# First phase of a two-layer encoder kernel: products from a host-transposed x, with the norm's row factor applied on the way out

## The chip, the cores and the metric

The kernel runs as one program on one core of a Trainium2 chip. The metric is the device time of one execution in microseconds (us). The engines named here are PE (TensorE, matrix products), ACT (ScalarE), DVE (VectorE), POOL (GpSimd) and SP (SyncE, which issues DMA transfers). A number such as L89 is a line of the kernel file.

## The reference, cut to what matters

Two layers over x of 256 rows and 1024 columns, float32. What the first phase computes is the RMSNorm ahead of the mixer and the first columns of the combined projection, q and k of the first head slot (three attention groups of one head each, 128 wide):

```python
for l in range(DEPTH):
    u = rms_norm(x, norm_mix_pre[l])          # x * rsqrt(mean(x*x) + eps) * gain
    m = hybrid_mixer(u, pos, w_in[l], ...)    # proj = u @ w_in; attention, Hyena branch, gates
    x = x + rms_norm(m, norm_mix_post[l])
    u = rms_norm(x, norm_ffn_pre[l])
    x = x + rms_norm(swiglu(u, w_gate_up[l], w_down[l]), norm_ffn_post[l])
```

The factor `rsqrt(mean(x*x) + eps)` is one number per row of x, so it is also one number per row of `u @ w`. The Hyena branch needs filters made by a small network with two sines, which don't depend on x: `h = sin(fr1*(z@w1+b1)); h = sin(fr2*(h@w2+b2)); h @ w3`.

## The kernel before, in words

Every product of the projections is made of three: weights and activations are split into a high part (ACT copies into a narrower format, `hi_of`, L86) and a low part (a subtraction, `lo_of`, L89, on DVE or POOL), and `mm3` (L80) multiplies high by high, high by low, low by high into one PSUM bank. Weights come in pieces of 128x768 or 128x1024 (`raw`, L140), one DMA each on SP's queue. `split_hi` makes `whi` of a piece on ACT, `split_lo` makes `wlo` of it on DVE (every fifth on POOL). Four buffers hold the newest `whi` and `wlo`; a further piece can be split only when PE has finished with an older one.

x sits in two tiles of 128 rows, X0 and X1. In the first phase x_rstd takes the sums of squares of a tile on ACT (L352) and the row factor on POOL (L359, L360); `pre_b` makes u = x * factor * gain on DVE (L385), with the gain row spread over the partitions by two PE products with ones (L813); `to_cols` transposes u on PE (L397) and splits the result into UH and UL, the activations with the model dimension on the partitions. Then `start` (L506) runs eight weight pieces of 128x768: q and k columns of head slot 0. It takes all eight for the rows of X0, makes u of X1 meanwhile, transposes it, and takes the eight pieces again for the rows of X1. Each piece and row tile is six products of 128x384.

After that `mixer` runs `slot(0)`: four more pieces for v of slot 0, each used for both row tiles (twelve products), then `slot(1)` with twelve pieces, and so on. After each piece `tick()` lets one or two background jobs issue their next step. The first two jobs are `filter_mlp` of the two layers. Their steps on PE are fixed by the order of the program: the first products (`fc`, L247) come after the first piece of slot 0, the second ones (`h`, L255) five ticks later, after the first piece of slot 1. Between them lies `sine` (L230): seven instructions on DVE (L233 to L242: `arg` and `kk`) and one on ACT (L243). Both layers' second products stand next to each other on PE.

PE runs in the order in which the program is written. In the block `ordered()` ACT, DVE and POOL do too; elsewhere a list scheduler sets the order of ACT, DVE, POOL and SP once, before the run, and each engine then works through its list in order.

## Time and profile before

| | |
|---|---|
| median of 3 runs | 1116.72 us (1114.47 to 1117.01) |
| the profiled execution | 1115.59 us |
| its span in the trace | 1113.8 us |
| PE busy | 1086.5 us (98%) |
| DVE, ACT, POOL busy | 702.8, 557.3, 411.5 us |
| mean DMA rate | 168 GB/s; 298 GB/s in the first 35 us |

The span runs from the first to the last instruction that the profile holds; the execution is 1.8 us longer. Times in rows are counted from the span's start. A row of the timeline has start, duration, engine, line, operation, output and inputs with shapes; in brackets stands how long the engine was idle before it, and what ended that. Products overlap, so that a row of 0.33 us stands 0.17 us behind the row before it; what a product costs is read from the distance of the starts.

### The profile page before, as it was taken

The numbers are of one execution on the slowest core, as the hardware profiler recorded it, in microseconds if no ns is written. First come the engines' busy times: TensorE is split into PE (matmuls) and PEld (weight loads), VectorE is DVE, ScalarE is ACT, GpSimd is POOL, SyncE is SP. The second block draws the span as 40 slices with busy tenths as digits, with TensorE's granted clock in tenths as the row PEclk, the third lists the DMA queues.
The fourth block names the chain that finished last, engine by engine and source line by source line (L and its number), as shares of the span: only waits on it lengthen the run. The fifth ranks groups of instructions, "written<-read, shape, count | busy, mean of one in ns | idle before, by whom it ended". The sixth has DMA issues, their size and how long they took to land.

```text
span 1113.8 us, 19545 instructions
## 1 busy us (share of the span) xinstructions
PE 1086.5 (98%) x7624; PEld 1039.8 (93%) x7624; DVE 702.8 (63%) x1128; ACT 557.3 (50%) x852; POOL 411.5 (37%) x499
## 2 busy tenths in 40 slices
PE   8999999999999999999989999999999999999997
PEld 7989999999898899998879999999999978999986
DVE  5789975555557756755574777865445676554554
ACT  6655554444545644544455464444355455544442
POOL 3665134478414224201126614455645321111110
PEclk9999999999999999999999999999999999999999
DMA  8575534344446555556654454444455556455662
GB/s 305 163 237 189 174 116 150 112 127 128 147 152 195 184 183 194 178 179 188 189 195 156 148 156 138 137 144 137 119 166 185 155 205 208 145 179 186 196 201 78
DMA packets 59878, 187.21 MB, mean 168 GB/s; under 512 B 6919, under 2 KB 9353, under 8 KB 59786
## 3 DMA queue, kind: packets, MB, share of 16 engines
q1 hardware_dynamic: 59786, 185.96, 52.8%
q8 instruction: 60, 0.98, 0.4%
q14 instruction: 32, 0.26, 0.1%
HBM read 184.89 MB, written 1.05 MB: 167 GB/s over the span
## 4 chain that ended last, share of the span: by engine, by line
PE 82%; POOL 5%; DVE 4%; DMA 3%; issue 3%; ACT 2%; SPq 0%; POOLq 0%; DVEq 0%; ACTq 0%
PE acc L78 79%; DMA gain<-in_gains_dram 2%; DVE wlo L89 1%; ACT whi L86 1%; DMA raw<-in_wa_dram 1%; PE acc L617 1%; POOL wlo L89 1%; ACT jk L352 1%; DVE X L373 1%; PE acc L397 1%; POOL GT L767 1%; PE acc L548 1%; PE acc L647 1%; POOL nr L360 0%; POOL sl L89 0%
## 5 line engine op out<-in xcount | busy, mean ns | idle before, releaser
L86 ACT ACTIVATE whi<-raw 128x1024 fp32r<-128x1024 f32 (+1 forms) x352 | 345.2, 989 | 380.2 <-PE acc L78 292.1
L89 DVE TENSOR_TENSOR wlo<-raw,whi 128x1024 fp32r<-128x1024 f32 (+1 forms) x291 | 346.3, 1195 | 233.4 <-ACT whi L86 232.5
L78 PE MATMUL acc<-UH,whi 128*128 128x256 f32 x1248 | 356.0, 285 | 0.0
L78 PE MATMUL acc<-UH,wlo 128*128 128x256 f32 x1248 | 353.1, 283 | 0.0
L78 PE MATMUL acc<-UL,whi 128*128 128x256 f32 x1248 | 353.0, 283 | 0.0
L89 POOL TENSOR_TENSOR wlo<-raw,whi 128x1024 fp32r<-128x1024 f32 (+1 forms) x61 | 138.4, 2269 | 401.0 <-ACT whi L86 401.0
L78 PEld LDWEIGHTS acc<-UL,whi 128*128 128x128 f32 x1248 | 239.3, 192 | 0.4
L78 PEld LDWEIGHTS acc<-UH,whi 128*128 128x128 f32 x1248 | 239.2, 192 | 0.4
L78 PEld LDWEIGHTS acc<-UH,wlo 128*128 128x128 f32 x1248 | 239.2, 192 | 0.0
L78 PE MATMUL acc<-wlo,UH 128*128 128x384 f32 x448 | 153.7, 343 | 5.4 <-DVE wlo L89 3.5
L78 PE MATMUL acc<-whi,UH 128*128 128x384 f32 x448 | 154.8, 346 | 0.0
L78 PE MATMUL acc<-whi,UL 128*128 128x384 f32 x448 | 152.3, 340 | 0.0
L78 PE MATMUL acc<-whi,hs 128*128 128x512 f32 x352 | 109.0, 389 | 0.0
L78 PEld LDWEIGHTS acc<-wlo,UH 128*128 128x128 f32 x448 | 85.8, 192 | 9.7 <-DVE wlo L89 6.0
L78 PEld LDWEIGHTS acc<-whi,UH 128*128 128x128 f32 x448 | 86.1, 192 | 1.3 <-ACT qk L668 0.4
L78 PEld LDWEIGHTS acc<-whi,UL 128*128 128x128 f32 x448 | 85.9, 192 | 0.2 <-DVE UL L89 0.2
L78 PEld LDWEIGHTS acc<-whi,hs 128*128 128x128 f32 x352 | 66.1, 188 | 13.6
L78 PE MATMUL acc<-wlo,hs 128*128 128x512 f32 x176 | 68.6, 390 | 0.5 <-DVE wlo L89 0.5
L799 DVE TENSOR_TENSOR HF<-acc,silu 128x256 f32<-128x256 f32 x38 | 16.1, 424 | 49.7 <-PE acc L78 49.7
L359 POOL TENSOR_SCALAR nv<-ss 128x1 f32<-128x1 f32 x16 | 4.8, 302 | 108.9 <-ACT jk L352 108.9
L78 PEld LDWEIGHTS acc<-wlo,hs 128*128 128x128 f32 x176 | 33.1, 188 | 7.7 <-DVE wlo L89 0.9
L565 POOL TENSOR_TENSOR t<-t 128x256 f32<-128x256 f32 x32 | 23.6, 741 | 38.8 <-DVE t L562 37.9
(164 smaller groups left out, 1688.3 us busy)
## 6 DMA issues: line engine op xcount, KB each, us to landing
raw<-in_wa_dram SPq DMA_DIRECT2D x240, 512.0 KB, 3.6
raw<-in_wq_dram SPq DMA_DIRECT2D x96, 384.0 KB, 3.2
raw<-in_wg_dram SPq DMA_DIRECT2D x16, 384.0 KB, 3.9
w<-in_w_dram SPq DMA_DIRECT2D x16, 256.0 KB, 4.6
gain<-in_gains_dram SPq DMA_DIRECT2D x7, 512.0 KB, 7.6
dec<-in_dec_dram SPq DMA_DIRECT2D x8, 256.0 KB, 4.2
bb<-in_hyb_dram SPq DMA_DIRECT2D x16, 128.0 KB, 3.7
dftraw<-in_dft_dram SPq DMA_DIRECT2D x3, 256.0 KB, 5.1
```

The lines of the kernel that those rows point to most:

```text
L78: nc.tensor.matmul(o, lT, r, start=start, stop=stop)
L86: return nc.scalar.activation(o, i, AF.Copy)
L89: (eng or nc.vector).tensor_tensor(o, i, h, op=OP.subtract)
L352: nc.scalar.activation(jk, half, AF.Square, scale=D ** -0.5, accum_out=ss[:, h:h + 1])
L373: stt(X[i][:, HALF[h]], t[h], r, X[i][:, HALF[h]], op0=OP.mult, op1=OP.add)
L397: nc.tensor.transpose(t[:, q * P:(q + 1) * P], u[:, h * 512 + q * P: h * 512 + (q + 1) * P], ident)
L548: nc.tensor.transpose(t[:, q * P:(q + 1) * P], eo[:, q // 2, q % 2, :], ident)
L565: ptt(t1[:, 0:256], t1[:, 0:256], t1[:, 256:512], op=OP.subtract)
L617: nc.tensor.transpose(t[:, q * P:(q + 1) * P], qk[i][:, j * 384 + g * P: j * 384 + (g + 1) * P], ident)
L647: nc.tensor.transpose(t[:, q * P:(q + 1) * P], S[:, i * 512 + q * P:i * 512 + (q + 1) * P], ident)
L767: ptt(g0, g0, ct(GT, 8 + c), op=OP.add)
L799: vtt(ct(HF, f), ob, sl, op=OP.mult)
```

## The change

x comes to the chip in two layouts. `xT`, transposed by the host (model dimension on the partitions, 1 MB), and `gT`, the gain as a column, are loaded on ACT's DMA queue at the very start. The first phase forms G = gain * xT, without the row factor, in two splits per 128 rows of the model dimension (ACT L525 for the high part with the gain as a scale operand, DVE L526 for the low part), and runs the eight pieces with G for both row tiles at once. The rows of the results of slot 0 (q, k, and v as well, which also uses G) get the row factor when ACT copies them out of PSUM. X0 and X1 themselves are loaded later, between the weight pieces, and their row factors are taken after pieces 5 and 6.

The normed U, which everything from slot 1 on needs, is built after the eight pieces: two DVE instructions put the row factors on a diagonal (`dg`), one PE product with a 128x128 of ones spreads them (`rb`), eight DVE instructions multiply xT, gain and factor (`ut`, L549), and four pairs of ACT and DVE instructions split them into UH and UL. The 16 transposes of u, the products that spread the gain row, and pre_b of the first phase go away.

```diff
-        grow = bigt(name="grow")[0:1]
-        nc.sync.dma_start(grow, a["gains"][0, 0:1])
-        for s in (slice(0, 512), slice(512, 1024)):
-            nc.sync.dma_start(X[0][:, s], a["x"][0:P, s])
-        ones = cst.tile([1, P], F32, name="ones")
+        gT = cst.tile([P, KT], F32, name="gT")
+        nc.scalar.dma_start(gT, a["gT"])
+        xT = [bigt(name="xT") for h in range(2)]
+        for q in range(4):
+            s = slice((q % 2) * 512, (q % 2) * 512 + 512)
+            nc.scalar.dma_start(xT[q // 2][:, s], a["xT"][:, q * 512:(q + 1) * 512])
+        ones = cst.tile([P, P], F32, name="ones")
...
+        def first_start():
+            G = new_U()
+            o = [[acc() for i in range(2)] for j in range(2)]
+            rs = []
...
+            with ordered():
+                for n in range(START):
+                    for k in (2 * n, 2 * n + 1) if n < 4 else ():
+                        gh = cols(G, k, 0)
+                        nc.scalar.activation(gh, xT_cols(k), AF.Copy, scale=gT[:, k:k + 1])
+                        stt(cols(G, k, 1), xT_cols(k), gT[:, k:k + 1], gh, op0=OP.mult, op1=OP.subtract)
+                    prefetch()
+                    if n == 3:
+                        prefetch()
+                    pc = piece(False)
+                    for i in range(2):
+                        rows_of(G, o[n // 4][i], i, pc, n % 4, 384)
+                    done(pc)
+                    if n in (5, 6):
+                        rs.append(x_rstd(n - 5))
+            dg = f256("dg")
+            for i in range(2):
+                nc.vector.tensor_scalar(dg[:, i * P:(i + 1) * P], ident, rs[i], None, op0=OP.mult)
+            t = acc()
+            mm(t[:, :L], ones, dg, True, True)
+            rb = f256("rb")
+            nc.scalar.activation(rb, t[:, :L], AF.Copy)
+            rb = rb[:, :].rearrange("p (i n) -> p i n", i=2)
+            U = new_U()
+            for k in range(0, KT, 2):
+                ut = t512("ut")
+                v = ut[:, :].rearrange("p (i k n) -> p i k n", i=2, k=2)
+                for q in range(2):
+                    stt(v[:, :, q, :], xT_cols(k + q), gT[:, k + q:k + q + 1], rb, op0=OP.mult, op1=OP.mult)
...
+                hi_of(uh, v)
+                lo_of(ul, v, uh)
+            return U, o, (G, rs)
...
-        def qkv_out(j, i, o, qk, vt):
+        def qkv_out(j, i, o, qk, vt, r=1.0):
             if j < 2:
                 w = slice(j * 384, (j + 1) * 384)
-                nc.scalar.activation(qk[i][:, w], o[:, :384], AF.Copy)
+                nc.scalar.activation(qk[i][:, w], o[:, :384], AF.Copy, scale=r)
...
-                            rows_of(U, o[i], i, pc, kk, 384)
+                            rows_of(G if G and not s else U, o[i], i, pc, kk, 384)
...
         for n in range(START):
             load(n >= RAW)
-            if n == 3:
-                nc.sync.dma_start(X[1], a["x"][P:2 * P, :])
+            if n in (5, 6):
+                nc.sync.dma_start(X[n - 5], a["x"][(n - 5) * P:(n - 4) * P, :])
         load_filter_consts()
         shared[0] = False
-        with ordered():
-            u0 = pre_b(0, x_rstd(0), g)
-            prefetch()
-            U = new_U()
-            to_cols(0, u0, U)
-            prefetch()
-            S = start(U, lambda: pre_b(1, x_rstd(1), g), 3)
+        U, S, first = first_start()
```

What stands in the engines' lists at the two places that the prediction speaks of follows. First DVE in the kernel before, from the last pieces split ahead of the filter networks on; `arg` and `kk` are the sine's tiles, and the number behind a name tells the buffers apart (arg_398 is layer 0's first sine, arg_411 layer 1's):

```order
L89 TENSOR_TENSOR wlo_424<-raw_421,whi_423 128x768
L89 TENSOR_TENSOR wlo_442<-raw_439,whi_441 128x768
L233 TENSOR_SCALAR arg_398<-acc_395,fpar_91 64x256
L235 TENSOR_SCALAR kk_400<-arg_398 64x256
L236 TENSOR_SCALAR kk_400<-kk_400 64x256
L241 SCALAR_TENSOR_TENSOR arg_398<-kk_400,arg_398 64x256 x3
L242 TENSOR_SCALAR arg_398<-arg_398 64x256
L233 TENSOR_SCALAR arg_411<-acc_408,fpar_91 64x256
L89 TENSOR_TENSOR wlo_460<-raw_457,whi_459 128x768
L235 TENSOR_SCALAR kk_413<-arg_411 64x256
L236 TENSOR_SCALAR kk_413<-kk_413 64x256
```

And the same engine in the changed kernel, from the first instruction of layer 0's sine to that of layer 1's second; the eight `ut` instructions of L549 stand directly ahead of these rows:

```order
L235 TENSOR_SCALAR arg_412<-acc_409,fpar_95 64x256
L89 TENSOR_TENSOR wlo_456<-raw_453,whi_455 128x768
L89 TENSOR_TENSOR UL_312<-ut_315,UH_311 128x2x256
L89 TENSOR_TENSOR dft_l_98<-dftraw_338,dft_h_97 128x512
L89 TENSOR_TENSOR UL_312<-ut_320,UH_311 128x2x256
L89 TENSOR_TENSOR UL_314<-ut_325,UH_313 128x2x256
L237 TENSOR_SCALAR kk_414<-arg_412 64x256
L89 TENSOR_TENSOR UL_314<-ut_330,UH_313 128x2x256
L89 TENSOR_TENSOR wlo_474<-raw_471,whi_473 128x768
L238 TENSOR_SCALAR kk_414<-kk_414 64x256
L243 SCALAR_TENSOR_TENSOR arg_412<-kk_414,arg_412 64x256 x3
L89 TENSOR_TENSOR wlo_551<-raw_548,whi_550 128x768
```

Behind these rows come the last step of arg_412, one more wlo, and the seven steps of arg_425, the sine of layer 1. The low parts of U and of the transform tables, which stood ahead of the first sine before, now stand inside it.

The other place is PE's list in the changed kernel at the second products of the filter networks, which stands as before between the first and the second piece of slot 1; h_411 and h_424 are the sines of layer 0 and layer 1:

```order
L78 MATMUL acc<-whi,UL 128x384
L78 MATMUL acc<-h_411,fc 128x256
L78 MATMUL acc<-h_424,fc 128x256
L78 MATMUL acc<-whi,UH 128x384
L78 MATMUL acc<-wlo,UH 128x384
```

Between the first products of these networks and these rows PE has the same four pieces as before. From about the hundredth instruction of each engine on, the lists of ACT, DVE, POOL, SP and PE hold the same operations in the same order as before.

## Rows read from the trace of the kernel before

**Rows 1.** The page's first part, the busy time of PE, and the waits of PE in the first 60 us (who waited for what, us in total, times, longest).

```profile
PE 1086.5 (98%) x7624; PEld 1039.8 (93%) x7624; DVE 702.8 (63%) x1128; ACT 557.3 (50%) x852; POOL 411.5 (37%) x499
...
PE acc L78 <- POOL sl L89: 2.2, 2, 1.7
PE acc L78 <- POOL wlo L89: 0.9, 1, 0.9
```

**Rows 2.** Busy time of the engines in three stretches: the eight pieces of the first phase; slot 0 and the first piece of slot 1 up to the end of the second filter products; the pieces after that. Columns: stretch, length, PE, PEld, DVE, ACT, POOL busy (and instructions), granted clock, DMA share, GB/s.

```profile
9.16:29.33 20.17, 19.30 (x105) 18.33 (x105) 14.44 (x17) 13.03 (x22) 8.33 (x12) 1.00 0.97 334
29.33:42.14 12.81, 12.81 (x70) 11.27 (x69) 9.84 (x18) 8.22 (x12) 9.90 (x21) 1.00 0.46 155
42.14:52.65 10.51, 10.51 (x61) 10.51 (x61) 8.90 (x20) 6.57 (x14) 4.38 (x11) 1.00 0.60 179
```

**Rows 3.** The timeline of the beginning, ACT, DVE and PE.

```profile
4.77 0.61 ACT L352 ACTIVATE jk<-X 128x512 bf16<-128x512 f32 x1
...
6.24 0.84 ACT L86 ACTIVATE whi<-raw 128x768 fp32r<-128x768 f32 x1 [0.77 <-DMA raw<-in_wq_dram]
...
7.88 0.95 DVE L89 TENSOR_TENSOR wlo<-raw,whi 128x768 fp32r<-128x768 f32 x1
...
9.16 0.69 PE L78 MATMUL acc<-whi,UH 128*128 128x384 f32 x1
...
12.03 0.34 PE L78 MATMUL acc<-whi,UL 128*128 128x384 f32 x1
```

**Rows 4.** SP's queue in the same time, one row of issues, and the DMA rate in one window (same columns as rows 2).

```profile
1.14 0.82 SPq L188 DMA_DIRECT2D X<-in_x_dram  x2
...
10.00:12.00 2.00, 2.00 (x7) 1.61 (x7) 1.96 (x3) 2.00 (x3) 0.00 (x0) 1.00 1.03 414
```

**Rows 5.** The timeline of PE and ACT from the first product of slot 0 to the first product after the second filter products, and one wait of PE's weight load between 30 and 45 us (the last row, columns as in rows 1).

```profile
29.33 0.33 PE L78 MATMUL acc<-whi,UH 128*128 128x384 f32 x1
31.24 0.34 PE L78 MATMUL acc<-whi,UL 128*128 128x384 f32 x1
31.51 1.07 PE L78 MATMUL acc<-fc 33*64 33x256 f32 x4
41.04 0.42 ACT L243 ACTIVATE h<-arg 64x256 f32<-64x256 f32 x1 [0.74 <-DVE arg L242]
41.05 1.16 PE L78 MATMUL acc<-h,fc 64*128 64x256 f32 x4
42.14 0.45 PE L78 MATMUL acc<-whi,UH 128*128 128x384 f32 x1
...
PEld acc L78 <- ACT h L243: 0.2, 1, 0.2
```

**Rows 6.** The timeline of DVE over the two first sines, and POOL's one low part in that time.

```profile
31.92 1.10 DVE L89 TENSOR_TENSOR wlo<-raw,whi 128x768 fp32r<-128x768 f32 x1 [3.87 <-ACT whi L86]
32.94 0.53 DVE L233 TENSOR_SCALAR arg<-acc,fpar 64x256 f32<-64x256 f32 x1
33.50 0.30 DVE L235 TENSOR_SCALAR kk<-arg 64x256 f32<-64x256 f32 x1
34.15 1.32 DVE L241 SCALAR_TENSOR_TENSOR arg<-kk,arg 64x256 f32<-64x256 f32 x3
35.51 0.29 DVE L242 TENSOR_SCALAR arg<-arg 64x256 f32<-64x256 f32 x1
37.77 2.86 DVE L241 SCALAR_TENSOR_TENSOR arg<-kk,arg 64x256 f32<-64x256 f32 x3
38.31 2.04 POOL L89 TENSOR_TENSOR wlo<-raw,whi 128x768 fp32r<-128x768 f32 x1 [1.04 <-ACT whi L86]
```

**Rows 7.** Groups of instructions by line and form (count, busy time, mean ns of one, then idle time before them).

```profile
L89 DVE TENSOR_TENSOR UL<-acc,UH 128x512 fp32r<-128x512 f32 x16 | 10.6, 687 | 1.0 <-ACT UH L86 0.6
L315 DVE TENSOR_TENSOR dd<-acc,dec 128x256 f32<-128x256 f32 x64 | 23.0, 411 | 1.0 <-PE acc L78 1.0
L385 DVE SCALAR_TENSOR_TENSOR u<-X,nr,acc 128x512 f32<-128x512 f32 x4 | 2.8, 744 | 6.5 <-POOL nr L360 6.5
L589 ACT ACTIVATE X<-acc,cw 128x256 f32<-128x256 f32 x32 | 17.6, 549 | 0.0
```

**Rows 8.** A place of layer 1 where PE waited: the timeline of PE, and the windows around it (same columns as rows 2).

```profile
576.64 0.34 PE L78 MATMUL acc<-whi,UH 128*128 128x384 f32 x1
578.23 0.57 PE L78 MATMUL acc<-wlo,UH 128*128 128x384 f32 x1 [1.25 <-DVE wlo L89]
578.60 0.52 PE L78 MATMUL acc<-whi,UL 128*128 128x384 f32 x1
581.48 0.49 PE L78 MATMUL acc<-whi,UL 128*128 128x384 f32 x1
...
576.00:578.00 2.00, 0.98 (x6) 0.66 (x4) 2.00 (x3) 1.32 (x4) 0.77 (x1) 1.00 0.60 169
578.00:580.00 2.00, 1.77 (x6) 1.76 (x7) 1.29 (x3) 2.00 (x5) 0.86 (x2) 0.60 0.44 112
580.00:582.00 2.00, 2.00 (x9) 1.91 (x8) 2.00 (x4) 0.32 (x1) 0.00 (x0) 0.55 0.72 206
```

More of the change, by code (lines that the diff above doesn't have):

```diff
@@ L504, in row_proj, with cols, xT_cols, start @@
                 return U, S
-        def start(U, second, at=0):
+        def first_start():
+            G = new_U()
+            o = [[acc() for i in range(2)] for j in range(2)]
+            rs = []
+            def cols(T, k, part):
+                return T[k // 4][part][:, :].rearrange("p (i k n) -> p i k n", i=2, k=4)[:, :, k % 4, :]
+            def xT_cols(k):
+                return xT[k // 4][:, (k % 4) * L:(k % 4 + 1) * L].rearrange("p (i n) -> p i n", i=2)
+            with ordered():
[27 more added lines that the diff above has]
+                    stt(v[:, :, q, :], xT_cols(k + q), gT[:, k + q:k + q + 1], rb, op0=OP.mult, op1=OP.mult)
+                uh, ul = (U[k // 4][part][:, :].rearrange("p (i k n) -> p i k n", i=2, k=4)[:, :, k % 4:k % 4 + 2, :]
+                          for part in range(2))
+                hi_of(uh, v)
+                lo_of(ul, v, uh)
+            return U, o, (G, rs)
+        def start(U, second):
             o = [[acc() for i in range(2)] for j in range(2)]
@@ L513, in start @@
                 rows_of(U, o[n // 4][0], 0, pcs[n], n % 4, 384)
-                if n == at:
+                if n == 0:
                     u1 = second()
@@ L663, in attend, with mixer @@
             yield
-        def qkv_out(j, i, o, qk, vt):
+        def qkv_out(j, i, o, qk, vt, r=1.0):
             if j < 2:
                 w = slice(j * 384, (j + 1) * 384)
-                nc.scalar.activation(qk[i][:, w], o[:, :384], AF.Copy)
+                nc.scalar.activation(qk[i][:, w], o[:, :384], AF.Copy, scale=r)
                 rotary(qk[i][:, w], i)
             else:
-                nc.scalar.activation(vt[:, i * 384:(i + 1) * 384], o[:, :384], AF.Copy)
-        def mixer(l, U, o, K):
+                nc.scalar.activation(vt[:, i * 384:(i + 1) * 384], o[:, :384], AF.Copy, scale=r)
+        def mixer(l, U, o, K, G=None, rs=(1.0, 1.0)):
             qk = [bigt(name="qk") for i in range(2)]
@@ L676, in mixer @@
                 for i in range(2):
-                    qkv_out(j, i, o[j][i], qk, None)
+                    qkv_out(j, i, o[j][i], qk, None, rs[i])
             OT = bigt(F32R, name="OTH"), bigt(F32R, name="OTL")
@@ L695, in slot @@
                     for i in range(2):
-                        qkv_out(j, i, o[i], qk, vt)
+                        qkv_out(j, i, o[i], qk, vt, 1.0 if s else rs[i])
                     tick()
@@ L808, in ffn @@
             return row_proj(l, NF, left, 3, (l + 1, 0) if l + 1 < DEPTH else None)
-        g = [acc() for h in range(2)]
-        for h in range(2):
-            mm(g[h], ones, grow[:, HALF[h]], True, True)
         for n in range(START):
             load(n >= RAW)
-            if n == 3:
-                nc.sync.dma_start(X[1], a["x"][P:2 * P, :])
+            if n in (5, 6):
+                nc.sync.dma_start(X[n - 5], a["x"][(n - 5) * P:(n - 4) * P, :])
         load_filter_consts()
         shared[0] = False
-        with ordered():
-            u0 = pre_b(0, x_rstd(0), g)
-            prefetch()
-            U = new_U()
-            to_cols(0, u0, U)
-            prefetch()
-            S = start(U, lambda: pre_b(1, x_rstd(1), g), 3)
+        U, S, first = first_start()
         shared[0] = True
@@ L832, in trunk @@
         for l in range(DEPTH):
-            U, S = mixer(l, U, S, K)
+            U, S = mixer(l, U, S, K, *(() if l else first))
             if l + 1 < DEPTH:
@@ L899, in _pack @@
     d["x"] = np.ascontiguousarray(i["x"][0][PERM])
+    d["xT"] = np.ascontiguousarray(d["x"].reshape(L, KT, P).transpose(2, 1, 0).reshape(P, KT * L))
+    d["gT"] = np.ascontiguousarray(i["norm_mix_pre"][0].reshape(KT, P).T)
     d["gains"] = np.stack([i["norm_mix_pre"], i["norm_mix_post"], i["norm_ffn_pre"], i["norm_ffn_post"]], 1)
```

## The prediction, on record before the result

> **What bounds the kernel now.** I read the page's first part first: PE is busy 98% of the span [rows 1], so time is won or lost only where PE's stream of products starts earlier, stands still or runs at a lower rate. Then the timeline of the beginning, because the change begins there: PE's first product of the projection starts at 9.16 us, after x, its row sums, u, the transposes and the first split [rows 3]. Then the windows by stage: the eight pieces of the first phase last from 9.16 to 29.33 us, slot 0 with the first piece of slot 1 and the second filter products until 42.14 [rows 2]. In that last stretch the waits matter most. PE's second filter products start at 41.05, and the sine that they read starts at 41.04; the weight load stood only 0.2 us for it [rows 5]. So the sine of the filter networks arrives just in time before: it has no slack. It is made on DVE, which ran through both sines from 31.92 us on, after standing idle for 3.87 us [rows 6].
>
> The question is thus two-sided: how much earlier does PE reach slot 0, and does DVE, which gets the building of U between slot 0's begin and the sines, still deliver the second sine in time?
>
> **Term 1, the first phase.** The first product now needs the first quarter of xT (128x512, 262 KB) and raw piece 0 (128x768, 393 KB), issued at the same time on two queues. Before, the two halves of X0 (524 KB) were there by 4.77 us and those with piece 0 (917 KB) at 6.24 [rows 3]; between these, 655 KB land at 4.77 + 131/393 x 1.47 = 5.3 us. The first issue of X stood at 1.14 us [rows 4], about where ACT's first of xT will stand, behind gT. Two scaled copies on ACT follow: a 128x256 instruction with operands for scale and bias takes 0.55 [rows 7], and the second starts before the first ends, so I take 0.9; then whi 0.84 and wlo 0.95 [rows 3]. The stream of products starts at 5.3 + 0.9 + 0.84 + 0.95 = 8.0 us. It has the same 96 products of 128x384. At full rate they stand (31.24 - 29.33)/11 = 0.174 us apart [rows 5]: 16.7 us. At its beginning PE ran slower before: eight products from 9.16 to 12.03 [rows 3], 2.87 instead of 1.39 us, and nothing has kept PE busy beforehand now, so I add 1.5. The end is 8.0 + 16.7 + 1.5 = 26.2; I use 26.1, as the first of the 96 runs ahead while wlo is made. Gone with the old order are eight transposes between the pieces and the wait of 0.9 for a low part on POOL [rows 1]. Each piece now serves twelve products (2.09 us) at once, so from the second on, a split (0.84 and 0.95) is ready in time even when a quarter of xT and a piece arrive together (655 KB at 414 GB/s [rows 4] is 1.6 us). Against 29.33 this is 3.2 us won. The product that spreads the factors costs about half of the 1.07 for the two first filter products [rows 5], 0.55. Won at the start of slot 0: 2.7 us.
>
> For the low end of this term, the first pair lands with X's second half at 4.77 and the copies take 0.6: 25.2. For the high end, the extra 1 MB of xT is paid in full ahead of the pieces, 1.05 MB at 414 GB/s, 2.5 us: 28.6. I stay near the low end because the later pieces are needed at only 393 KB in 2.09 us, half of what the window shows.
>
> The trace has all transfers on one queue, so it doesn't show how two share. The Trainium skill, DMA: Bandwidth & Descriptors, section "Issuing engines are not separate DMA queues", says that transfers issued by several engines run on the same 16 DMA engines and interleave, and that a second issuer saves only issue time. No run here shows it yet. By that rule the pair lands together, as I reckon; were ACT's queue an addition, the pair could land some 0.5 us earlier.
>
> **Term 2, from slot 0 to the second filter products.** Count from the end of the first phase, T = 26.1. PE itself reaches the second filter products at T + 0.55 + 5 x 2.09 + 1.1 = T + 12.1, or 38.2: five pieces and the first filter products. DVE's list decides whether it may go on. Piece 11's whi can only be made when the last piece of the first phase is finished, for it takes its buffer: whi 0.84, wlo 0.95, T + 1.8. Then, in order: eight `ut` of 128x256 at 0.37 (128x512 takes 0.74 for one [rows 7], so half; 0.41 for another 128x256 instruction is the upper bound), 3.0; first step of the sine 0.53, wlo 0.95; low parts of U and of the tables, five at 0.69 [rows 7], 3.45; one kk 0.30, wlo 0.95, kk 0.30, three steps 1.32, wlo 0.95, 0.29, wlo 0.95 [rows 6]. With 13.0 that is T + 14.8. The second sine adds 0.53 + 0.30 + 0.30 + 1.32 + 0.29 = 2.7: T + 17.5. During such a stretch POOL makes a low part, and beside it the same three steps of a sine took 2.86 instead of 1.32 [rows 6]; the list has one such low part and the rotary steps there again, so I add 1.5: T + 19.0. ACT's sine 0.42, then the second layer's product 0.55 [rows 5]: T + 20.0 = 46.1. Before, the next piece began at 42.14 [rows 5]. So PE is 4.0 us later than before, though it came to slot 0 2.7 us earlier: the wait for the sine eats 6.7 us.
>
> The bounds of this term: no collision with POOL, 0 instead of 1.5; two of them, 3.0; `ut` 0.41 each, 0.3 more. The removed transposes and u give DVE and ACT nothing back here, since both stood ahead of slot 0. The row factor as a scale in the six copies of q, k and v costs less than the 0.55 that an ACT instruction with such operands takes in all [rows 7], and PE's wait covers it. On ACT whi of piece 15 stands behind the two copies of v, which end T + 11.8, so its wlo starts by T + 12.7: within the list's own pace. Rows from PSUM, `dg` and the issue of gT hide under the first phase.
>
> **Term 3, PE's rate after the wait.** Where PE had been busy only 0.98 of 2 us (576 to 578), the granted clock of the next two windows was 0.60 and 0.55, and products stood 0.32 us apart instead of 0.174 until 581.48 [rows 8]: the lower of the two levels, 1.2 GHz. Eleven products cost 11 x 0.146 = 1.6 us. In the wait of term 2 PE does one small product in some 7 us, a longer rest than that. I take 1.6; bounds 0 and 2.2.
>
> The Trainium skill, TensorE: Matmul & The Clock Gate, section "Part 1: The HAM clock gate", says that 1.2 GHz is the default and that only sustained activity releases 2.4. Rows 8 agree (0.55 after a stretch half idle). The rule speaks against this change twice: at the start, where there are no products with ones and no transposes ahead of the stream, and here; by it the sum below holds, without it the sum would be 4.0.
>
> **The sum.** Later: 4.0 + 1.6 = 5.6 us. From there on the lists are the same as before, PE is the bound, and I find nothing that gives time back, except the 2.2 us that PE waits for low parts on POOL between 50 and 60 us [rows 1]: this work hangs on q and k of slot 1, which ACT copies out after the second sines, so I let the wait stand. The profiled execution took 1115.59 us (span 1113.8): 1115.6 + 5.6 = 1121.2. The median of the runs shown is 1.1 above that execution, so I forecast 1122.3, say 1122 us.
>
> **Rivals.** Changes under 0.3% (3.35 us, so 1113.4 to 1120.1) can't be told from none.
>
> 1. The sine is late, but PE gets part of it back: clock not lowered (4.0), or the waits for POOL shrink (down to 4.0 - 2.2 = 1.8). Time 1118.5 to 1120.7, mostly "same". For it: such waits exist [rows 1]. Against: rows 8. Chance 0.21.
> 2. Not slower: DVE keeps ahead of PE. The place is DVE's list between T and layer 1's second-to-last step; the price is the 6.7 us wait; the point from which it decides is the second sine ready at T + 12.1. Then the 2.7 us of term 1 survive: 1114.0, and with the waits for POOL gone too, 1111.8. For it: DVE idled 3.87 us at 28 to 32 [rows 6], and a higher start of the list would use that. Against: the list alone sums to T + 17.5 without any collision. Chance 0.17, half of it beyond 0.3%.
> 3. The first phase starves: xT, eight pieces and X share one pool of transfers, and the end comes at 28.6 instead of 26.1, all else alike: 5.6 + 2.5 = 8.1, 1124.8. For it: DMA share 0.97 in the first phase [rows 2]. Against: the spread of demand in term 1. Chance 0.14.
>
> The forecast itself has 0.48. It and rival 3 make slower 0.62, with some of rival 1's upper end 0.66; same is most of rival 1 and half of rival 2, 0.25; faster 0.09. The range leaves out rival 2's better half and the far end of rival 3 with both collisions: 1115 to 1126.5. The likeliest case alone has 1120.5 to 1124.
>
> **What would show it.** First product after splitting near 7 us, stream from 8.0; slot 0's first product near 26.6 instead of 29.33; then PE's largest wait of the first 60 us, by far, on ACT h, at the second filter products, with DVE full from T + 2 until that sine; the next piece near 46 with products 0.32 apart and a granted clock near 0.6. If PE doesn't wait there, I am wrong in sign; if the stream begins after 10 us, term 1 is wrong.

## The result and the profile after

| | before | after |
|---|---|---|
| median | 1114.72 us (6 runs, 1113.38 to 1117.01) | 1121.82 us (6 runs, 1121.19 to 1123.81) |
| ratio | | 1.0070, 95% interval 1.0055 to 1.0084 |
| the profiled execution's span | 1113.8 us | 1119.7 us |

The runs of before stand beside those of after in the same comparison. The change makes the kernel 7.1 us slower. The spans of the two profiled executions stand 5.9 us apart.

I read the profile in the order of the prediction. First the page's first part and the waits of PE in the first 60 us (who waited for what, us in total, times, longest), which answer to [rows 1]:

```profile
PE 1082.6 (97%) x7606; PEld 1038.6 (93%) x7606; DVE 705.1 (63%) x1141; ACT 561.6 (50%) x861; POOL 415.4 (37%) x500
...
PE acc L78 <- ACT h L245: 8.0, 2, 4.2
```

PE is busy for 3.9 us less than before, and yet the kernel takes longer: PE stands still. By far its largest wait after the start is the predicted one, for `h`, the sine, twice about 4 us.

The timeline of the beginning of ACT and PE (ACTq is ACT's DMA queue) and of the end of the first phase, beside [rows 3]:

```profile
1.16 3.50 ACTq L190 DMA_DIRECT2D xT<-in_xT_dram  x4
4.69 1.28 ACT L525 ACT_TABLE_LOAD   x1 [4.69 <-DMA gT<-in_gT_dram]
6.59 0.91 ACT L525 ACTIVATE UH<-xT,gT 128x256 fp32r<-128x256 f32 x2 [0.62 <-DMA xT<-in_xT_dram]
7.41 0.83 ACT L86 ACTIVATE whi<-raw 128x768 fp32r<-128x768 f32 x1
...
8.29 0.69 PE L78 MATMUL acc<-whi,UH 128*128 128x384 f32 x1 [8.29 <-ACT whi L86]
9.28 0.69 PE L78 MATMUL acc<-wlo,UH 128*128 128x384 f32 x1 [0.30 <-DVE wlo L89]
...
27.88 0.59 PE L78 MATMUL acc<-dg,ones 128*128 128x256 f32 x2
28.12 0.53 PE L78 MATMUL acc<-whi,UH 128*128 128x384 f32 x1
```

The first copy from xT stands at 6.59 us, where ACT waited for the transfer. The stream of products starts at 9.28, and slot 0 at 28.12 instead of 29.33 [rows 5]: 1.2 us are won.

The timeline of DVE, ACT and PE from there to the piece after the second filter products, beside [rows 5, 6]:

```profile
30.21 3.25 DVE L549 SCALAR_TENSOR_TENSOR ut<-xT,gT,rb 128x256 f32<-128x256 f32 x8
33.37 0.54 DVE L235 TENSOR_SCALAR arg<-acc,fpar 64x256 f32<-64x256 f32 x1
37.31 0.68 DVE L89 TENSOR_TENSOR UL<-ut,UH 128x512 fp32r<-128x512 f32 x1
39.09 2.17 DVE L243 SCALAR_TENSOR_TENSOR arg<-kk,arg 64x256 f32<-64x256 f32 x3
44.76 2.81 DVE L243 SCALAR_TENSOR_TENSOR arg<-kk,arg 64x256 f32<-64x256 f32 x3
...
43.46 0.42 ACT L245 ACTIVATE h<-arg 64x256 f32<-64x256 f32 x1
48.40 0.42 ACT L245 ACTIVATE h<-arg 64x256 f32<-64x256 f32 x1 [4.52 <-DVE arg L244]
...
43.93 0.75 PE L78 MATMUL acc<-h,fc 64*128 64x256 f32 x2 [3.82 <-ACT h L245]
48.87 1.22 PE L78 MATMUL acc<-h,fc 64*128 64x256 f32 x2 [4.18 <-ACT h L245]
50.02 0.69 PE L78 MATMUL acc<-whi,UH 128*128 128x384 f32 x1
```

DVE has no gap worth naming from 28.38 us on: `ut`, the first step of layer 0's sine, the low parts of U, and only then the rest of that sine. The first sine starts on ACT at 43.46, the second at 48.40 (the second before: 41.04 [rows 5]), and the next piece starts at 50.02 instead of 42.14 [rows 5]: 7.9 us later, from a slot that began 1.2 earlier.

The windows of the two stages and of the time behind the wait (columns as in [rows 2]):

```profile
8.29:28.12 19.83, 19.52 (x98) 19.10 (x99) 10.20 (x16) 12.90 (x24) 5.39 (x6) 1.00 0.91 315
28.12:50.02 21.90, 13.89 (x71) 11.64 (x69) 21.01 (x38) 13.72 (x23) 13.41 (x19) 0.87 0.61 202
50.00:55.00 5.00, 5.00 (x17) 4.99 (x17) 3.79 (x10) 1.88 (x4) 3.79 (x12) 0.53 0.19 74
```

In the second stage DVE is busy 21.0 of 21.9 us (before 9.84 of 12.81 [rows 2]) and PE 13.9. After the wait the granted clock is 0.53, and the products stand 0.32 us apart until 54.66. There PE is 10.0 us behind the kernel before, which is 2.1 more.

POOL's timeline shows what I had not reckoned with. First the kernel before, with the issue of the filter weights `w` on SP's queue (SPq) and their first use on POOL (`sd`), then the kernel after:

```profile
17.61 0.43 SPq L284 DMA_DIRECT2D w<-in_w_dram  x1
...
23.59 0.73 POOL L296 TENSOR_TENSOR sd<-w 128x256 f32<-128x256 f32 x1 [6.57 <-DMA w<-in_w_dram]
```

```profile
20.08 9.62 SPq L140 DMA_DIRECT2D raw<-in_wq_dram  x5
...
31.17 0.42 SPq L286 DMA_DIRECT2D w<-in_w_dram  x1
...
36.60 3.06 POOL L298 TENSOR_TENSOR sd<-w 128x256 f32<-128x256 f32 x1 [9.87 <-DVE UL L89]
44.51 1.87 POOL L89 TENSOR_TENSOR wlo<-raw,whi 128x768 fp32r<-128x768 f32 x1
```

The transfer of `w` was issued at 17.61 us before and is issued at 31.17 after: on SP's queue it now stands behind five weight pieces, which SP issues from 20.08 to 29.70 us with waits in between. It lands 5.3 us after its issue, at 36.5, and POOL, idle for 9.87 us, starts `sd` at 36.60. The row names a low part of U on DVE, which also ended just then and released a buffer (`ut`, `w`, `sd` and the raw tables share one pool of seven, t512); but `sd` could not have started more than 0.1 us sooner without it, since `w` was not there. Why SP's list has `w` so late is not shown; in the run without U it is issued at 20.30. POOL's `sd`, the rotary steps and its low part of a piece, which ran from 23.6 to 40.4 us before, all fall into the time of the sines.

### The profile page after: what moved, and what is told of

The parts are those of the page before. It is cut to its first block, busy times and chain, and to the rows that moved or that the text cites. A ratio compares the mean times of both kernels' runs of the same rounds, so it can differ in the third digit from the quotient of the medians.

```text
span 1119.7 us, 19540 instructions
## 1 busy us (share of the span) xinstructions
PE 1082.6 (97%) x7606; PEld 1038.6 (93%) x7606; DVE 705.1 (63%) x1141; ACT 561.6 (50%) x861; POOL 415.4 (37%) x500
## 4 chain that ended last, share of the span: by engine, by line
PE 82%; POOL 5%; DVE 4%; DMA 3%; ACT 3%; issue 2%; SPq 0%; POOLq 0%; DVEq 0%; ACTq 0%
PE acc L78 79%; DMA gain<-in_gains_dram 2%; DVE wlo L89 1%; ACT whi L86 1%; DMA raw<-in_wa_dram 1%; PE acc L667 1%; DVE X L375 1%; ACT jk L354 1%; POOL wlo L89 1%; POOL GT L818 1%; PE acc L697 1%; PE acc L598 1%; POOL sl L89 1%; PE acc L399 1%; DMA xT<-in_xT_dram 0%
## 5 line engine op out<-in xcount | busy, mean ns | idle before, releaser
L78 PEld LDWEIGHTS acc<-whi,hs 128*128 128x128 f32 x352 | 66.1, 188 | 13.6
```

The costliest lines, as they stand in the source:

```text
L78: nc.tensor.matmul(o, lT, r, start=start, stop=stop)
```

## The experiments

Times are medians. Each batch had its own runs of the kernel before beside it (1114.57, 1113.95, 1114.56 and 1114.96 us), and the ratios are to these. A shift is the difference between the starts of one and the same product of PE in two traces. Four theories are weighed: that U's instructions on DVE ahead of the sines are the cause (list), that what is taken away there comes back as another wait (given on), that the steps of the second sine are torn apart by low parts of pieces (chain), and that the transfers of two queues cost the late start (sharing).

### No U at all

This run leaves out the row factor from slot 1 of layer 0 on: G takes the place of U, and `dg`, its product, `ut` and the splits of U are not there.

```diff
-            dg = f256("dg")
...
-                hi_of(uh, v)
-                lo_of(ul, v, uh)
-            return U, o, (G, rs)
+            return G, o, (G, rs)
```

> The changed kernel without the building of U (dg, its product, rb, eight ut, four high and four low parts); all later products of layer 0 use G, so the row factor of the norm is left out there. Theory: DVE's list is 6.5 us shorter ahead of layer 1's sine, the wait of 8.0 us for ACT h falls to 0 to 2 us, the low clock goes: 1111 to 1114 us. Rival A (start and transfers): below 1 us of change, 1121. Rival B: 1118 to 1121.

Measured: 1116.03 us (12 runs), ratio 1.0009 (0.9996 to 1.0023). The waits of PE in its first 60 us:

```profile
PE acc L78 <- POOL wlo L89: 2.5, 1, 2.5
PE acc L78 <- ACT h L245: 0.6, 1, 0.6
```

The wait for the sine falls from 8.0 to 0.6 us, and the kernel stands 1.5 us above the median of its own runs of before instead of 7.1. The transfer of `w` is issued at 20.30 here and POOL starts `sd` at 27.85, so that this run takes away both effects of U at once, the load on DVE and the late `w`. It also shows the other side: the time is not the 1111 to 1114 us that I expected, and even without any U no gain over the kernel before is seen. The 1.2 us won at slot 0 (here 2.0) go into a wait of 2.5 us for a low part on POOL at 33.5 us and the lower clock behind it.

### The second filter products later

Four ticks are put between the first and the second products of both networks.

```diff
             sine(h1, p1[:64, :L], 64, fpar[:, l, :], 0)
+            for _ in range(4):
+                yield
             yield
```

> The changed kernel with the second filter products moved four background steps (some 8.4 us of PE's work) later in PE's list; nothing is left out. Theory (layer 1's sine is late because DVE builds U ahead of it): PE's wait of 8.0 us for ACT h falls below 1 us, the low clock after it goes, and the time falls by 8 to 10 us, to 1112 to 1114 us, at or a little under the kernel before. Rival A (the 1 MB of xT and the start cost the time): no change, 1121 to 1122. Rival B (DVE is short over the whole stretch from 30 to 70 us, whatever the order): the wait comes back at the filter products with gst, 1118 to 1121.

Measured: 1128.04 us, ratio 1.0117 (1.0096 to 1.0139). The waits of PE up to 140 us:

```profile
PE acc L78 <- POOL wlo L89: 5.9, 1, 5.9
PE acc L78 <- POOL sl L89: 3.8, 1, 3.8
PE acc L78 <- DVE dl L89: 2.4, 3, 1.0
```

The wait for the sine is gone, as wanted, and 12.1 us of other waits stand in this stretch, where the changed kernel has 2.0 besides those for the sine. The first stands at 48.48 us, for the low part of the piece that POOL splits. In the changed kernel this low part was ready at 46.38 us [the row of 44.51 above], and PE came to its piece, the second behind the wait, only at 54.02: the wait for the sine had hidden it. My expectation had looked at DVE alone. POOL's first `sd` in this run stands after an idle time of the same length as in the changed kernel, and here the row names the transfer:

```profile
36.81 3.48 POOL L300 TENSOR_TENSOR sd<-w 128x256 f32<-128x256 f32 x1 [9.87 <-DMA w<-in_w_dram]
```

### Both sines ahead of U

The filter networks' first step is taken ahead of `dg`.

```diff
+            queue.extend(filter_mlp(l) for l in range(DEPTH))
+            tick()
             dg = f256("dg")
...
-        queue.extend(filter_mlp(l) for l in range(DEPTH))
```

> The changed kernel with the first filter products right behind the eight pieces, ahead of dg, so that DVE makes both sines first and then U; nothing is left out. Theory: the sines (5.4 us on DVE) are ready before PE wants them, no wait for ACT h; U is now late, and PE waits 2 to 4 us for UH or UL at the first piece of slot 1: 1115 to 1118 us. Rival B (DVE's sum alone decides, not the order): PE waits as long for U as it did for h, some 8 us, 1120 to 1122. Rival A: 1121 to 1122.

Measured: 1126.70 us, ratio 1.0103 (1.0084 to 1.0122). The timeline of PE where it waited:

```profile
36.58 1.22 PE L78 MATMUL acc<-dg,ones 128*128 128x256 f32 x2 [6.82 <-DVE dg L540]
48.27 1.13 PE L78 MATMUL acc<-h,fc 64*128 64x256 f32 x4
...
57.96 0.69 PE L78 MATMUL acc<-wlo,UH 128*128 128x384 f32 x1 [4.02 <-POOL wlo L89]
```

PE works in program order, so now it stands 6.8 us for `dg`, which is behind the sines on DVE, and 4.0 us for POOL's low part; the second filter products (48.27) don't wait at all. The waits have only changed their names, and the time is longer than any of the three expectations had it.

### PE kept busy in the wait

Ahead of each second product PE gets 17 products of 128x512, whose results the true product overwrites.

```diff
             p2 = acc()
+            for _ in range(17):
+                mm(p2, dft_h[:, 0, :], dft_h[:, :, :].rearrange("p a b -> p (a b)"), True, True)
             mm(p2[:, :L], fw2[:, l, :], h1, True, True)
```

> The changed kernel with 17 idle products of 128x512 on a constant table ahead of each of the two second filter products, about 3.7 us each, in the time in which PE waits (results are overwritten, nothing is left out). Theory on the clock: PE's rest is what lowers it, so the next piece runs at 0.174 us per product instead of 0.32, and the time falls by the 2.0 us that these 14 products lost: 1119 to 1120.5 us, with h as late as before. Rival: the clock falls for another cause, or the idle products delay the real ones: 1121.5 to 1123.

Measured: 1122.48 us, ratio 1.0063 (1.0044 to 1.0082). Windows of this run, and one of the changed kernel:

```profile
46.00:48.00 2.00, 2.00 (x10) 1.65 (x10) 1.97 (x2) 0.00 (x0) 2.00 (x3) 1.00 0.00 0
50.00:55.00 5.00, 5.00 (x28) 4.59 (x28) 4.22 (x11) 1.91 (x5) 5.00 (x15) 1.00 0.44 163
66.00:68.00 2.00, 1.32 (x3) 1.06 (x4) 2.00 (x3) 0.00 (x0) 0.62 (x1) 0.71 0.82 299
```

```profile
66.00:68.00 2.00, 0.41 (x3) 0.03 (x1) 2.00 (x2) 0.84 (x1) 2.00 (x2) 1.00 0.63 128
```

The mechanism of term 3 is shown: with PE busy the granted clock stays at 1.00, and from 50.02 to 54.66 us of the changed kernel PE gains 2.1 us on it (shift +0.69 to -1.42). The total doesn't follow. The stream began 1.0 us later in this run (9.25 for the first product), and at 66.68 PE waits for a low part on POOL (1.9 us), as in the changed kernel at 68.07 (1.7 us). Behind it the clock falls to 0.71 here and stays at 1.00 there, and between these waits and 71 us 1.5 us are lost again.

### All transfers of the start on one queue

gT and the quarters of xT go to SP's queue, each quarter ahead of the weight piece that goes with it.

```diff
-        nc.scalar.dma_start(gT, a["gT"])
+        nc.sync.dma_start(gT, a["gT"])
...
         for n in range(START):
+            if n < 4:
+                s = slice((n % 2) * 512, (n % 2) * 512 + 512)
+                nc.sync.dma_start(xT[n // 2][:, s], a["xT"][:, n * 512:(n + 1) * 512])
             load(n >= RAW)
```

> The changed kernel, with gT and the four quarters of xT issued on SP's queue, each ahead of the weight piece that goes with it. Theory sharing (the stream of products began at 9.28 us instead of the 8.0 that I reckoned, because four quarters of xT on ACT's queue and eight pieces on SP's share the same transfers, so that the first pair lands late, at 6.59): the first pair lands by 5.4, the stream begins near 8.0, slot 0 at 26.8 instead of 28.12, and as DVE's list starts as much earlier, the whole gain of 1.3 stays: about 1120.5. Theory volume (the same bytes must land whatever the queue; the first quarter is late because of the first issue and the latency): stream again at 9.0 to 9.5, time 1121.5 to 1122.5.

Measured: 1122.15 us, ratio 1.0072 (1.0054 to 1.0090). The timeline of ACT and PE at its beginning:

```profile
5.67 1.28 ACT L522 ACT_TABLE_LOAD   x1 [5.67 <-DMA xT<-in_xT_dram]
6.97 0.91 ACT L522 ACTIVATE UH<-xT,gT 128x256 fp32r<-128x256 f32 x2
...
9.65 0.69 PE L78 MATMUL acc<-wlo,UH 128*128 128x384 f32 x1 [0.31 <-DVE wlo L89]
```

Half of the theory holds. The first quarter of xT is there at 5.67 us instead of 6.59, so the order on two queues did delay it by 0.9. But ACT loads its table only now, behind the transfer. In the changed kernel the table load started at 4.69, when gT had landed, and was over before xT came. Here it stands on the path with its 1.28 us, and the stream starts at 9.65, later than 9.28. (Slot 0 starts at 27.96 all the same, 0.2 us earlier, since fewer products stood at the slow spacing.)

### Only layer 1's second product later, and U's low parts on POOL

Two further attempts to relieve DVE or PE. The first is the delay by four ticks for layer 1's network alone; the second gives the four low parts of U to POOL.

```diff
+            for _ in range(4 * l):
+                yield
```

```diff
-                lo_of(ul, v, uh)
+                lo_of(ul, v, uh, nc.gpsimd)
```

> The changed kernel, with the second products of layer 1's filter network alone put four ticks later on PE; those of layer 0 stay. Theory list (PE loses what DVE's list ahead of each sine is too long; what is taken out of PE's way is won): PE still waits 3.8 us for layer 0's sine, the second wait of 4.2 goes, the next piece starts near 45.8 instead of 50.02, time about 1117.6. Theory given on (DVE and POOL are both full between 30 and 60 us, and what is not waited for at the sine is waited for a little later, as in the run that moved both networks): no wait for the second sine, but new waits of 3 to 5 us for low parts on POOL between 50 and 70 us, time 1120 to 1125.

> The changed kernel, with the four low parts of U made on POOL, which stands idle from 26.7 to 36.6 us, instead of on DVE. Theory list: DVE's list ahead of layer 0's sine is 2.8 us shorter, PE's wait falls from 8.0 to about 5, time about 1119. Theory given on: POOL's low parts of U slow DVE's instructions beside them, or push POOL's own list back, so that the wait for the sine falls by less than 1.5 or waits for low parts on POOL come in its place: 1120.5 to 1124.

Measured: 1125.54 us for the first, ratio 1.0107 (1.0089 to 1.0125). PE waits 3.8 us for the first sine and no longer for the second, and the next piece starts at 45.12, 4.9 us earlier, as the list theory has it. But then PE waits 4.2 us for `sh`, a split that ACT makes behind the sine that follows the moved product, and 0.8 for POOL: at 65.5 us it has started as many products as the changed kernel, and the lead is gone.

For the second: 1123.66 us, ratio 1.0087 (1.0069 to 1.0105). DVE is rid of 2.8 us, and the first sine is not earlier: PE's product of it starts at 44.21 instead of 43.93. Its timeline of DVE and POOL:

```profile
38.84 1.38 DVE L238 TENSOR_SCALAR kk<-kk 64x256 f32<-64x256 f32 x1
40.26 3.11 DVE L243 SCALAR_TENSOR_TENSOR arg<-kk,arg 64x256 f32<-64x256 f32 x3
...
35.50 5.86 POOL L89 TENSOR_TENSOR UL<-ut,UH 128x512 fp32r<-128x512 f32 x3 [1.75 <-ACT UH L86]
```

Beside POOL's low parts of U a step of the sine takes 1.38 us instead of 0.28, and three steps beside the last of them and the `sd` that follows take 3.11 instead of 1.32 [rows 6]. What DVE is spared comes back as slower instructions.

### U inside the first phase, three ways

DVE stands idle from 23.9 to 28.4 us in the changed kernel, while both row factors are known at 22.9. So the product that spreads them can stand earlier on PE, if X is loaded two pieces sooner. First try: the product behind piece 5, U in two halves behind pieces 5 and 6, each step in turn (`ut`, high part, low part). Second: only the product moves, ahead of piece 6, and the list places U. Third: the product ahead of piece 5, U in halves behind pieces 5 and 7, and one more weight piece split ahead. The third's core:

```diff
+                    if n == 5:
+                        prefetch()
+                        dg = f256("dg")
...
+                        mm(t[:, :L], ones, dg, True, True)
                     pc = piece(False)
...
+                    if n == 5:
...
+                        make_U((0, 2), rb, U)
+                    if n in (3, 4):
+                        rs.append(x_rstd(n - 3))
+                    if n == 7:
+                        make_U((4, 6), rb, U)
...
-            if n in (5, 6):
-                nc.sync.dma_start(X[n - 5], a["x"][(n - 5) * P:(n - 4) * P, :])
+            if n in (3, 4):
+                nc.sync.dma_start(X[n - 3], a["x"][(n - 3) * P:(n - 2) * P, :])
```

> The changed kernel, with the same U built inside the first phase, where DVE stands idle for 4.5 us and more: X is loaded after pieces 3 and 4 instead of 5 and 6, the row factors are taken after pieces 3 and 4, the product that spreads them stands after piece 5, and U is made in two halves behind pieces 5 and 6. Nothing is left out; only the place of DVE's and ACT's instructions of U moves, and one product of PE. Theory list (U's place on DVE, behind the phase and ahead of the sines, is the cause): the wait for the sine falls under 1 us, the next piece starts at 40.5 to 41.5 instead of 50.02, and the time is 1112 to 1116, as in the run without U or better. Theory given on (DVE and POOL are full from 30 to 60 us whatever stands where): other waits, for low parts, take its place, and the time stays at 1119 or above.

> The changed kernel, with X loaded after pieces 3 and 4, the row factors taken there, and the product that spreads them ahead of piece 6 on PE instead of behind the phase; the instructions of U stay where the list puts them, now in front of the sines, with ACT's splits of the weight pieces up to piece 10 ahead of them. Theory list (what stands on DVE ahead of the sines decides, if nothing that PE needs is pushed back): ut starts near 25 instead of 30.2 us, the low parts of U are done by 33, the first sine is ready near 39 and the second near 43.5, PE waits about 3 instead of 8.0, time 1116 to 1118.5. Theory given on (other waits take the place of what is removed): 1119.5 to 1124.

> As the run with U inside the first phase, but with the split of the next weight pieces always ahead of U on ACT and DVE: the product of the row factors stands ahead of piece 5, one more piece is split ahead there, the first half of U is made behind piece 5 and the second behind piece 7. Theory list, mended: what failed in the first try was the order (PE waited 4.2 us in all for whi behind UH and rb, and ran at the lower clock for 16 us after it); with the pieces first there is no wait for whi, slot 0 starts by 28.3, only two low parts of U stand among the sines, PE waits 0 to 3 us for the second sine, and the time is 1114 to 1117. Theory given on: the time stays above 1119, whatever the order, since other waits come, for low parts on POOL or for whi.

The first try: 1125.09 us, ratio 1.0100 (1.0079 to 1.0120). The wait for the sine is gone altogether, and the time is worse. Two rows of PE's timeline, and a window behind them, show where it went:

```profile
29.86 0.44 PE L78 MATMUL acc<-whi,UH 128*128 128x384 f32 x1 [2.94 <-ACT whi L86]
35.28 0.69 PE L78 MATMUL acc<-whi,UH 128*128 128x384 f32 x1 [1.30 <-ACT whi L86]
```

```profile
40.00:42.00 2.00, 2.00 (x6) 0.76 (x5) 0.84 (x3) 1.78 (x2) 2.00 (x3) 0.50 0.39 146
```

ACT had the splits of the next pieces behind its copies for U, each of which waits for DVE. PE waited 4.2 us for `whi`, and ran at the lower clock from about 31 to 45.6 us. This was a fault of my order, not a verdict on the theory.

The second: 1119.54 us (11 runs), ratio 1.0036 (1.0024 to 1.0049). `ut` starts at 25.04 instead of 30.21, and PE waits 6.1 us for the sines instead of 8.0 (read in the profiled execution, which at 1123.47 us was the slowest of the eleven). The interval lies below that of the changed kernel: U's place does cost time. DVE's list is not the only thing that moved, though: `w` is issued at 25.35 here instead of 31.17. The third: 1120.10 us, ratio 1.0047 (1.0027 to 1.0067), 5.7 us of waits for the sines. In both most of the wait is for the second sine (4.0 and 4.4 us). The timeline of DVE and of PE in the third:

```profile
40.48 0.97 DVE L89 TENSOR_TENSOR wlo<-raw,whi 128x768 fp32r<-128x768 f32 x1 [0.24 <-ACT whi L86]
42.94 1.11 DVE L89 TENSOR_TENSOR wlo<-raw,whi 128x768 fp32r<-128x768 f32 x1 [1.06 <-ACT whi L86]
43.98 2.44 DVE L243 SCALAR_TENSOR_TENSOR arg<-kk,arg 64x256 f32<-64x256 f32 x2
...
42.23 0.70 PE L78 MATMUL acc<-h,fc 64*128 64x256 f32 x2 [1.37 <-ACT h L245]
47.30 1.22 PE L78 MATMUL acc<-h,fc 64*128 64x256 f32 x2 [4.37 <-ACT h L245]
```

Two low parts stand between the steps of the second sine, and both wait for a split of ACT; two steps that follow are slowed beside POOL.

### The sines whole

One piece is split ahead of each sine, and the low parts of the pieces that follow are held behind what was written before them. Once with U inside the first phase (third way), once with U where the change has it.

```diff
+                if 13 <= count[1] <= 16 and not share:
+                    tc.keep_in_program_order(
+                        nc.vector.tensor_tensor(lo[:, :n], raw[:, :n], h[:, :n], op=OP.subtract))
...
+            prefetch()
             sine(h1, p1[:64, :L], 64, fpar[:, l, :], 0)
```

> The second run with U inside the first phase, and in addition each of the two first sines whole on DVE: one weight piece is split ahead of each sine, and the low parts of pieces 12 and 13 may not be taken between the steps of a sine (they stand behind the first and behind the second). Theory chain (after U is out of the way, what makes the second sine late is the low parts that the list puts between its steps, which wait for ACT's splits): first sine ready by 36.5 to 37.5, second by 40 to 42.5, PE waits 0 to 1.5 instead of 5.7, the next piece starts at 42 to 43.5 instead of 48.45, no stretch at the lower clock behind it, time 1113.5 to 1116.5. Theory given on: the waits move to the low part of piece 12 or 13 or to POOL, the time stays at 1118 or above.

> The changed kernel with U where it was, behind the phase, and only the sines made whole on DVE (pieces 12 and 13 may not be taken between their steps). Theory chain and list together: the eight ut and four low parts of U still stand ahead of the first sine, which is ready near 40.5; the low part of piece 12 comes at 41.5, where PE wanted it at 37.6, so PE waits some 3.5 us there and 0.5 to 1.5 for the second sine, in all 4 to 5 instead of 8.0; time 1117.5 to 1119. If U's place were no cause at all, this run would be as fast as its companion with U inside the phase; if the order of the sines' steps were no cause, it would stay at 1121 to 1123.

With U inside: 1121.00 us, ratio 1.0058 (1.0042 to 1.0075). Rows of DVE and PE:

```profile
52.85 0.96 DVE L166 TENSOR_TENSOR wlo<-raw,whi 128x768 fp32r<-128x768 f32 x1
...
40.13 0.70 PE L78 MATMUL acc<-h,fc 64*128 64x256 f32 x2
42.37 0.70 PE L78 MATMUL acc<-h,fc 64*128 64x256 f32 x2 [1.55 <-ACT h L249]
53.87 0.65 PE L78 MATMUL acc<-wlo,UH 128*128 128x384 f32 x1 [3.78 <-DVE wlo L166]
```

Up to the second filter products the chain theory holds to its numbers: the first sine is in time, the second costs 1.5 us, and PE's product of it is 0.8 us behind the kernel before, where the changed kernel was 7.3 behind. Its "no stretch at the lower clock" fails: behind this wait the products stand 0.32 us apart again from 43.6 to 46.5 us, and with 0.7 us of waiting for POOL's low part the shift goes from +0.9 to +3.2 us. Then a fault of my edit: the hold reached to piece 15 instead of 13, so that this piece's low part came to stand behind the second-stage sines of both networks (52.85), PE waited 3.8 us for it and fell to the lower clock once more, and the shift went from +3.2 to +8.7 us. That the time is above 1118 is what "given on" had said, but this wait was of my making, and what the version without it takes was not run.

With U behind the phase: 1125.54 us, ratio 1.0100 (1.0080 to 1.0120). The second sine costs PE only 0.7 us, the first none, but the low part of a piece behind the first sine costs 2.7 us at 41.53, POOL's low part 2.9 at 52.49, and the held one 2.9 at 59.56. It misses the 1117.5 to 1119 that I had expected; the first of the waits was as foreseen, and the other two were not.

## Why the prediction was right, and where its terms were off

The direction, the place and the size were right: the forecast was 1122 and the median is 1121.8. The deciding step, that DVE gets U between the first phase and the sines and can't hide it, is shown by the run without U (1.5 us above the kernel before instead of 7.1) and by the run that only makes U's row factors ready earlier (ratio 1.0036 against 1.0070). In both `w` is issued earlier as well, so they don't tell DVE's own list from POOL's work beside it. Term by term:

- **Term 1, 2.7 us won, was 1.2.** Two sizes failed. The step "these land at 5.3 us": the first quarter of xT was there at 6.59. From then on my chain of two copies, whi and wlo held (predicted 2.69, measured 9.28 - 6.59 = 2.69). The run with one queue had it at 5.67. It bears on the rule that I had cited from the Trainium skill, DMA: Bandwidth & Descriptors, section "Issuing engines are not separate DMA queues": the transfers of two issuers interleave. The traces agree with it, and they add what I had missed, that the quarter needed first shares with transfers that are not: weight piece 0, issued at 0.72, landed at 4.1, and the quarter, issued at 1.16 behind gT, landed only at 6.6, next to piece 1 (issued at 1.17, landed at 6.4). The second size is the slow beginning: it lasted over 14 products from 9.28 us on instead of eight before, and the stream took 18.6 us (9.28 to 27.88) instead of 18.1. The spreading product cost 0.24, not 0.55. The end of the phase, 27.88, lay nearer to rival 3's 28.6 than to my 26.1.
- **Term 2, next piece at T + 20.0, was T + 22.1.** The list of instructions was right one by one (eight `ut` took 3.25 for 3.0). I had taken one collision with POOL, 1.5 us, and 3.0 as the bound for two; there were two, at 39.09 (2.17 instead of 1.32) and at 44.76 (2.81, and 0.70 for the last step), 2.8 us together. The step that failed is the count of POOL's work: I had it as "one such low part and the rotary steps there again", and did not see that the transfer of `w` moves behind five weight pieces on SP's queue, so that all of POOL's list moves into the sines. The rest is the lower clock, at which the last two filter products took 1.15 us (48.87 to 50.02) instead of 0.55. That the late transfer is what delays POOL is read from its landing (36.5 us, `sd` at 36.60); a run with U where the change has it and `w` issued as early as before was not made. By the rows alone the collisions are the smaller part: without their 2.8 us DVE would still end the second sine at T + 17.7, with PE ready for it at T + 12.2.
- **Term 3, 1.6 us for the clock, was 2.1**, 14 products instead of eleven. The run with PE kept busy shows the mechanism and its size.
- **The sum.** 5.6 us predicted; at 54.66 us it was 10.0. So 4.1 us came back later, while I had written "I find nothing that gives time back", except for the waits for POOL, which I let stand: 0.5 by 63 us, as waits for POOL are shorter, 3.4 about the border of the layers (566 to 625 us), and the rest in small steps. Of the 3.4, 1.5 is a fall of the clock at 616 to 620 us that the profiled run of before had and that of after had not. Over the medians, 7.1 us apart, less came back. The forecast thus came out near by some luck: a too small loss up to 54.66 us and a gain that I did not see lay against each other, and the forecast of the total stands on the median of three runs, 1116.72, where six gave 1114.72. In differences, 5.6 us were forecast and 7.1 measured.

Of the rivals, the second (DVE keeps ahead) falls, and its price with it: even with no U at all the time is 1.5 us above the kernel before, not 2.7 to 4.9 below it. What was won at slot 0 went there into 2.5 us of waiting for a low part on POOL ahead of the sines. The first was right in that something is given back.

## What to carry to other kernels

Work that is moved off the start of a kernel lands somewhere: ask not only how long it takes on its engine, but which transfers change their place in a queue with it, and which engine's work moves with these (here `w`, from 17.6 to 31.2 us, and POOL's work into the sines). Where several late chains end at nearly the same time, taking one wait away shows the next; before an edit, read when the others are ready (here POOL's low part, ready at 46.4 us and asked for at 54.3, behind the wait). An engine that takes instructions strictly in order needs the short chain that another engine waits for in one piece, ahead of work that itself waits.

## What the runs showed of the hardware

- The granted clock column doesn't show the slow start: it reads 1.00 from 8 to 14 us in the changed kernel, while products stand 0.32 us apart until about 13.6. At the same spacing behind the later wait it reads 0.53.
- Two waits of nearly the same length at the same product were answered differently: 1.66 us with the clock left at 1.00, 1.89 us with a fall to 0.71.
- DVE and POOL slow each other down when both work, and by how much depends on POOL's instruction: three steps of a sine took 1.32 us beside small rotary steps of 128x48, and 2.17, 2.81 and 3.11 where `sd` or a low part stood beside them; POOL's first `sd` took 3.06 instead of 0.73 us.
- ACT's first table load (1.28 us) can stand behind a transfer: it started at 4.69 us in the changed kernel, when gT was there, and at 5.67 with one queue, when the first quarter of xT was. It adds 1.28 us to the path when nothing else is waited for in that time.
